# Feed-forward weights packed in alternating runs and read by a 4-D pattern

## The chip, the cores and the metric

The kernel runs on one core of one Trainium2 chip. The metric is the device time of one execution in microseconds; the number shown for the kernel before is the median of three runs. Beside the runs one execution was recorded by the hardware profiler, and all rows below come from that one.

## The reference

A sequence of 256 tokens of width 1024 goes through four layers of a mixer (banded attention, gated linear attention, differential attention, banded attention again) and a feed-forward part, each followed by a layer norm, and then through a second block with two more feed-forward parts, a sparse-attention and convolution mixer and a cross attention. The change touches only the feed-forward part of three of the four layers of the first block:

```
def swiglu(x, w_gate_up, w_down):
    g, u = jnp.split(x @ w_gate_up, 2, axis=-1)
    return (jax.nn.silu(g) * u) @ w_down
...
    for i in range(DEPTH):
...
        h = layer_norm(DN_ALPHA * h + y, ln1_g[i], ln1_b[i])
        h = layer_norm(DN_ALPHA * h + swiglu(h, ffn_w_gate_up[i], ffn_w_down[i]), ln2_g[i], ln2_b[i])
```

Here x is 256 x 1024, w_gate_up is 1024 x 5632 (2816 columns of gate, 2816 of up) and w_down is 2816 x 1024, all in float32.

## The kernel before

All weights are read from one flat array in DRAM, which the host packs in the order of use (`pack_weights`). A unit of the plan is either of kind "in" (eight row tiles of 128 x 512 of a weight matrix, for x @ W) or of kind "out" (up to four row tiles of 128 x 1024, for the projection back to 1024). A unit is used in quarters of 1024 floats per partition. SP loads each quarter into a buffer `raw`; ScalarE (L268) rounds it into `wh`, of type float32r, and VectorE (L269) writes the rest, `wl` = raw - wh. An activation is likewise held as a high and a low part (`sth`, `stl` for a layer's input, `gth`, `gtl` for the gated hidden values), transposed, so that it can be the stationary operand.

Each product is then three matmuls into one PSUM bank (`mm3`): wh with the high activation (L280), wl with the high activation (L282), wh with the low activation (L284). The weights are the moving operand, 512 columns for each matmul:

```
        for o, w in zip(outs, whs):
            nc.tensor.matmul(o, xh, w, start=first, stop=False)
```

`lin` does this for the "in" units into a bank `lin`, `lin_out` for the "out" units into two banks `acc`, one for each half of the 1024 columns. In the feed-forward part of a layer there are 11 "in" units (5 of gate, 5 of up, and one that has the last 256 columns of both) and 22 row tiles of w_down. The two token tiles of 128 go through the network as two streams that use the same split weights, the second some quarters behind the first.

The order on each engine is set by a planner at the end of the file: it plays all instructions through with rough durations that depend on the number of elements and on the engine, takes the most urgent ready one, and hands the order to the framework, which draws the waits.

The keys of the units of the layers' feed-forward parts are of the form ((i, "f"), kind, j), with i the layer; those of other units have a string or a plain number in the first place.

## Time and profile before

| | |
|---|---|
| median of 3 runs | 1971.57 us (1969.64 to 1972.45) |
| profiled execution, from its first to its last instruction | 1969.9 us |
| PE (TensorE matmuls) busy | 1945.0 us, 99% |
| DVE (VectorE) busy | 1169.3 us, 59% |
| ACT (ScalarE) busy | 927.4 us, 47% |
| DMA, weights | 607 transfers of up to 512 KB, 175 GB/s over the span |

[...] What a matmul takes away from the others is the distance between starts, and a row of a timeline gives the start in its first column. "xN" rows of a timeline merge N instructions. [...]

The feed-forward parts of layers 1, 2 and 3 stand, with a little of the neighbouring work of the other token tile between them, at 454.8 to 654 us, 767.6 to 968 us and 1083.7 to 1281.6 us of the span.

### The profile page before, as it was taken

Reading aid. Unit: us, or ns where it says so; the run is one execution under the profiler, and the core shown is the slowest. Engines: PE = TensorE matmul, PEld = TensorE weight load, DVE = VectorE, ACT = ScalarE, POOL = GpSimd, SP = SyncE. Lnnn points to the kernel's source line nnn. Section 1 sums busy time; section 2 is a strip of 40 time slices with the busy share of each in tenths; the row PEclk is TensorE's granted clock in tenths of the full one; section 3 lists DMA queues with packets and bytes.
Section 4 is the critical chain, followed back from the end, with each engine's and each line's share of the span. In section 5 each row is a group of like instructions: output and inputs, shape, how many; then the busy total and the mean of one; then the engine's idle time right before and its main releaser. Section 6 shows DMA issues by size and latency. Waiting matters only on the chain.

```text
span 1969.9 us, 23888 instructions
## 1 busy us (share of the span) xinstructions
PE 1945.0 (99%) x8998; PEld 1546.9 (79%) x8998; DVE 1169.3 (59%) x1687; ACT 927.4 (47%) x1332; POOL 48.6 (2%) x71
## 2 busy tenths in 40 slices
PE   8999999999999999999999999999999999999998
PEld 6788887678888777888877888878887788788886
DVE  5566456557555768545755655664467857556454
ACT  5445445444444555444554444444444545555442
POOL 0000000000000000000000000000001000000000
PEclk9999999999999999999999999999999999999999
DMA  9436555645555434655543655465545355536562
GB/s 287 150 139 209 181 191 154 193 148 198 186 183 182 171 129 162 222 183 181 183 143 135 217 186 184 150 225 181 186 171 183 113 197 193 163 116 206 180 186 70
DMA packets 103293, 345.59 MB, mean 175 GB/s; under 512 B 13369, under 2 KB 20473, under 8 KB 103178
## 3 DMA queue, kind: packets, MB, share of 16 engines
q1 hardware_dynamic: 103178, 344.07, 51.7%
q8 instruction: 70, 1.15, 0.2%
q14 instruction: 45, 0.37, 0.1%
HBM read 341.01 MB, written 3.01 MB: 175 GB/s over the span
## 4 chain that ended last, share of the span: by engine, by line
PE 95%; DMA 2%; DVE 1%; ACT 1%; issue 0%; SPq 0%; DVEq 0%; POOLq 0%; ACTq 0%
PE lin L282 19%; PE lin L280 19%; PE lin L284 19%; PE acc L282 9%; PE acc L284 9%; PE acc L280 9%; PE at L326 4%; PE at L574 2%; PE lin L662 1%; PE at L599 1%; DMA raw<-in_weights_dram 1%; DMA toep<-t 1%; PE lin L753 0%; PE at L741 0%; PE lin L951 0%; DVE wl L269 0%
## 5 line engine op out<-in xcount | busy, mean ns | idle before, releaser
L269 DVE TENSOR_TENSOR wl<-raw,wh 128x1024 fp32r<-128x1024 f32 (+2 forms) x614 | 741.8, 1216 | 459.6 <-ACT wh L268 459.0
L268 ACT ACTIVATE wh<-raw 128x1024 fp32r<-128x1024 f32 (+2 forms) x614 | 644.7, 1053 | 680.9 <-PE lin L284 437.6
L280 PE MATMUL lin<-wh,sth 128*128 128x512 f32 x1696 | 677.1, 403 | 3.2 <-ACT sth L331 1.4
L282 PE MATMUL lin<-wl,sth 128*128 128x512 f32 x1696 | 671.5, 400 | 1.7 <-DVE wl L269 1.7
L284 PE MATMUL lin<-wh,stl 128*128 128x512 f32 x1696 | 669.1, 399 | 0.0
L280 PEld LDWEIGHTS lin<-wh,sth 128*128 128x128 f32 x1696 | 319.5, 188 | 78.7 <-issue 4.0
L284 PEld LDWEIGHTS lin<-wh,stl 128*128 128x128 f32 x1696 | 319.3, 188 | 77.5 <-issue 4.9
L282 PEld LDWEIGHTS lin<-wl,sth 128*128 128x128 f32 x1696 | 319.4, 189 | 76.8 <-issue 4.8
L282 PE MATMUL acc<-wl,gth 128*128 128x512 f32 x752 | 251.7, 401 | 0.1
L280 PE MATMUL acc<-wh,gth 128*128 128x512 f32 x752 | 248.5, 399 | 0.2 <-ACT gth L331 0.2
L284 PE MATMUL acc<-wh,gtl 128*128 128x512 f32 x752 | 248.3, 398 | 0.0
L284 PEld LDWEIGHTS acc<-wh,gtl 128*128 128x128 f32 x752 | 141.2, 188 | 33.7 <-issue 1.3
L282 PEld LDWEIGHTS acc<-wl,gth 128*128 128x128 f32 x752 | 140.8, 189 | 32.5 <-issue 1.4
L280 PEld LDWEIGHTS acc<-wh,gth 128*128 128x128 f32 x752 | 139.8, 188 | 31.9 <-issue 1.0
L326 PE MATMUL at<-ident,t 128*128 128x128 f32 x604 | 100.4, 273 | 4.5 <-DVE t L534 1.5
L326 PEld LDWEIGHTS at<-ident,t 128*128 128x128 f32 x604 | 75.2, 140 | 28.3 <-ACT t L613 4.1
L331 ACT ACTIVATE gth<-at 128x512 fp32r<-128x512 f32 (+1 forms) x98 | 55.4, 566 | 65.8 <-PE at L326 65.7
L555 DVE TENSOR_TENSOR t<-t,lin 128x512 f32<-128x512 f32 x60 | 41.2, 687 | 74.7 <-PE lin L284 74.7
L347 POOL TENSOR_TENSOR sm<-sm,mhalf 128x1 f32<-128x1 f32 (+2 forms) x42 | 35.8, 852 | 1672.6 <-DVE sm L474 952.1
L332 DVE TENSOR_TENSOR gtl<-at,gth 128x512 fp32r<-128x512 f32 (+1 forms) x98 | 64.1, 654 | 20.2 <-ACT gth L331 17.0
L585 ACT ACTIVATE p<-p,sm 128x128 f32<-128x128 f32 (+1 forms) x112 | 49.6, 444 | 52.4 <-DVE sm L583 52.4
L552 ACT ACTIVATE t<-lin 128x512 f32<-128x512 f32 x60 | 35.9, 598 | 49.8 <-PE lin L284 49.5
(158 smaller groups left out, 911.2 us busy)
## 6 DMA issues: line engine op xcount, KB each, us to landing
raw<-in_weights_dram SPq DMA_DIRECT2D x607, 512.0 KB, 3.5
b<-toep SPq DMA_DIRECT2D x40, 128.0 KB, 4.1
bc<-in_ln_g_dram SPq DMA_DIRECT2D x8, 512.0 KB, 3.7
bc<-in_ln_b_dram SPq DMA_DIRECT2D x8, 512.0 KB, 5.9
toep<-t SPq DMA_DIRECT2D x2, 768.0 KB, 10.4
bc<-in_ffn_post_g_dram SPq DMA_DIRECT2D x2, 512.0 KB, 3.6
p<-in_mem_dram SPq DMA_DIRECT2D x2, 512.0 KB, 6.6
out_dram<-h SPq DMA_DIRECT2D x4, 256.0 KB, 2.0
```

What stands on the lines that cost most here:

```text
L268: nc.scalar.activation(hi[:, c], src[:, c], AF.Copy)
L269: nc.vector.tensor_sub(lo[:, c], src[:, c], hi[:, c].bitcast(F32))
L280: nc.tensor.matmul(o, xh, w, start=first, stop=False)
L282: nc.tensor.matmul(o, xh, w, start=False, stop=False)
L284: nc.tensor.matmul(o, xl, w, start=False, stop=last)
L326: self.nc.tensor.transpose(b[:, k], src[:, k * 128:(k + 1) * 128], self.ident)
L331: self.nc.scalar.activation(hi, b[:, :n], AF.Copy)
L332: self.nc.vector.tensor_sub(lo, b[:, :n], hi.bitcast(F32))
L552: nc.scalar.activation(gate[j], acc, AF.Silu)
L555: nc.vector.tensor_mul(s, s, acc)
L574: nc.tensor.matmul(banks[e][:, i, :nk], qT[ps, pr, :], kT(ps, pr, nk), start=True, stop=True)
L585: nc.scalar.activation(P[:, hh, :nk], P[:, hh, :nk], AF.Exp, bias=nm[:, hh:hh + 1], accum_out=sm[:, hh:hh + 1])
```

## The change

For the units whose key belongs to the feed-forward part of layer 1, 2 or 3 the host permutes the columns of each block of 512 before it writes the flat array: the block is cut into runs of 4 (layer 1), 16 (layer 2) or 2 floats (layer 3), the even runs go to its first 256 columns and the odd runs to its last 256. On the chip the moving operand of these matmuls is read by a pattern of four dimensions (partition, run pair, half, place in the run), which takes a run from the first half, then a run from the second half, and so on, so that the array sees the columns in their natural order. The transfers, the splits, the stationary operands and the outputs keep their shapes. Comments are also taken out, which moves line numbers: L280, L282 and L284 become L298, L300 and L302.

```
+RUN = {1: 4, 2: 16, 3: 2}
+
+
+def run_of(key):
+    return RUN.get(key[0][0], 0) if isinstance(key, tuple) and isinstance(key[0], tuple) else 0
+
+
+def halved(m, run):
+
+    return m.reshape(m.shape[:-1] + (-1, 256 // run, 2, run)).swapaxes(-3, -2).reshape(m.shape)
...
         blk = blk.reshape(128, -1)
+        if run_of(key):
+            blk = halved(blk, run_of(key))
         n = u.qcols * u.dma_q
...
-    def mm3(self, outs, xh, xl, whs, wls, first, last):
+    def mm3(self, outs, xh, xl, whs, wls, first, last, run=0):
         nc = self.nc
+        if run:
+            whs, wls = ([w.rearrange("p (h g j) -> p g h j", h=2, j=run) for w in ws] for ws in (whs, wls))
+            outs = [o.rearrange("p (g h j) -> p g h j", h=2, j=run) for o in outs]
...
-                self.mm3([acc[:, :n]], st[0][:, kt], st[1][:, kt], [wh[:, s]], [wl[:, s]], kt == 0, kt == 7)
+                self.mm3([acc[:, :n]], st[0][:, kt], st[1][:, kt], [wh[:, s]], [wl[:, s]], kt == 0, kt == 7,
+                         run_of(key))
...
-                self.mm3_out(gt, a, accs, c, wh, wl, first and a == 0, last and a == u.nq - 1)
+                self.mm3_out(gt, a, accs, c, wh, wl, first and a == 0, last and a == u.nq - 1, run_of(key))
...
-    def mm3_out(self, gt, a, accs, c, wh, wl, first, last):
+    def mm3_out(self, gt, a, accs, c, wh, wl, first, last, run):
...
-                 first, last)
+                 first, last, run)
```

In the built program the moving operand of the changed matmuls has, behind the partitions, the steps and counts [4, 64] [256, 2] [1, 4] in layer 1, [16, 16] [256, 2] [1, 16] in layer 2 and [2, 128] [256, 2] [1, 2] in layer 3, in floats; the output, whose four dimensions lie one behind the other, is again one run of 512. The order of instructions on each of the five engines is the one of before. Only PE has new waits: at 27 places, 9 in each of the three layers, the first matmul into a `lin` bank now also waits for a count of PE's own semaphore.

The following rows are PE's at the first use of a run of 2, before; the `lin` banks are PSUM banks of the two token tiles, `sth` and `stl` the high and low part of their input.

```order
L284 MATMUL lin_8983<-wh_8986,stl_1881_8638 128x512
L280 MATMUL lin_9014<-wh_8871,sth_1914_8784 128x512
L282 MATMUL lin_9014<-wl_8872,sth_1914_8784 128x512
L284 MATMUL lin_9014<-wh_8871,stl_1915_8785 128x512
L280 MATMUL lin_9014<-wh_8871,sth_1914_8784 128x512
L282 MATMUL lin_9014<-wl_8872,sth_1914_8784 128x512
```

And these stand there now, with the one wait that is new.

```order
L302 MATMUL lin_8983<-wh_8986,stl_1881_8638 128x512
L298 MATMUL lin_9014<-wh_8871,sth_1914_8784 128x512 [waits PE_49]
L300 MATMUL lin_9014<-wl_8872,sth_1914_8784 128x512
L302 MATMUL lin_9014<-wh_8871,stl_1915_8785 128x512
L298 MATMUL lin_9014<-wh_8871,sth_1914_8784 128x512
L300 MATMUL lin_9014<-wl_8872,sth_1914_8784 128x512
```

No instruction has moved; the wait is for an earlier matmul of the same engine, by the counts of the built program 29 matmuls back at this place, and 11, 29 or 40 back at the 27 places.

## Rows read from the trace of the kernel before

**Rows 1.** Page: busy us per engine, then busy tenths and clock by slices.
```profile
PE 1945.0 (99%) x8998; PEld 1546.9 (79%) x8998; DVE 1169.3 (59%) x1687; ACT 927.4 (47%) x1332; POOL 48.6 (2%) x71
...
PE   8999999999999999999999999999999999999998
...
PEclk9999999999999999999999999999999999999999
```

**Rows 2.** Windows of the three stretches: width, busy (count) by engine, clock, DMA.
```profile
core 0: us, PE busy (x) PEld busy (x) DVE busy (x) ACT busy (x) POOL busy (x), PEclk, DMA share, GB/s
454.00:654.00 200.00, 200.00 (x895) 161.82 (x894) 117.00 (x125) 89.37 (x100) 1.48 (x2) 1.00 0.53 187
767.00:968.00 201.00, 201.00 (x898) 162.42 (x897) 117.06 (x124) 89.91 (x100) 1.92 (x2) 1.00 0.54 189
1083.00:1282.00 199.00, 199.00 (x889) 160.89 (x888) 115.48 (x125) 90.54 (x104) 3.44 (x3) 1.00 0.52 184
```

**Rows 3.** Waits of PE, whole span: us in total, times, longest.
```profile
PE at L326 <- DMA h<-in_x_dram: 5.0, 2, 3.8
PE at L599 <- ACT p L585: 2.3, 1, 2.3
PE lin L282 <- DVE wl L269: 1.7, 3, 1.0
```

**Rows 4.** Timeline of PE in the first stretch: start, duration.
```profile
575.66 0.40 PE L280 MATMUL lin<-wh,sth 128*128 128x512 f32 x1
575.90 0.39 PE L282 MATMUL lin<-wl,sth 128*128 128x512 f32 x1
576.13 0.40 PE L284 MATMUL lin<-wh,stl 128*128 128x512 f32 x1
576.36 0.39 PE L280 MATMUL lin<-wh,sth 128*128 128x512 f32 x1
```

**Rows 5.** Timeline of PE just before 48 us.
```profile
46.00 0.63 PE L282 MATMUL lin<-wl,sth 128*128 128x512 f32 x1
46.42 0.63 PE L284 MATMUL lin<-wh,stl 128*128 128x512 f32 x1
46.85 0.63 PE L280 MATMUL lin<-wh,sth 128*128 128x512 f32 x1
47.28 0.63 PE L282 MATMUL lin<-wl,sth 128*128 128x512 f32 x1
```

**Rows 6.** Windows around those matmuls.
```profile
44.00:48.00 4.00, 4.00 (x14) 2.58 (x13) 2.51 (x7) 3.17 (x5) 0.00 (x0) 0.57 1.03 411
48.00:52.00 4.00, 4.00 (x28) 3.52 (x28) 3.04 (x8) 3.36 (x11) 0.00 (x0) 1.00 0.95 360
```

**Rows 7.** Timeline of PE where matmuls have 200 columns.
```profile
1493.73 0.26 PE L282 MATMUL lin<-wl,sth 128*128 128x200 f32 x1
1493.83 0.28 PE L284 MATMUL lin<-wh,stl 128*128 128x200 f32 x1
1493.93 0.28 PE L280 MATMUL lin<-wh,sth 128*128 128x200 f32 x1
```

**Rows 8.** Groups by form, DVE and ACT: count, busy us, mean ns, idle before.
```profile
L787 DVE TENSOR_TENSOR t<-lin,cst 128x256 f32<-128x256 f32 x8 | 3.1, 414 | 0.0
L608 DVE COPY pt<-at 128x256 f32<-128x256 f32 x2 | 0.9, 426 | 0.1
...
L606 ACT ACTIVATE k<-at 128x512 f32<-128x512 f32 x12 | 7.1, 592 | 3.9 <-PE at L326 3.8
L606 ACT ACTIVATE pt<-at 128x512 f32<-128x512 f32 x20 | 11.9, 593 | 13.6 <-PE at L599 9.3 <-PE at L326 4.2
```

## The prediction

> **What bounds the kernel now.** I read the page first. PE is busy for 1945.0 of 1969.9 us and in every one of the 40 slices at eight or nine tenths, at the full granted clock [rows 1]; the reader is to see that no other engine comes near (DVE has 59%). A share over the whole span says little about a stage, so the busy time by stretch comes next: in the three stretches that hold the changed feed-forward parts PE is busy for all of 200, 201 and 199 us, at granted clock 1.00, while DVE is busy for 115 to 117 us and ACT for some 90 us of each, and the DMA engines for little more than half [rows 2]. The view of waits says the same from the other side: over the whole span PE's longest sums of waiting are 5.0, 2.3 and 1.7 us [rows 3], and within the three stretches it lists none. So here a nanosecond that a matmul loses lengthens the kernel by a nanosecond, and nothing that SP, ACT or DVE gains shows at all.

> What a matmul costs is the distance between two starts. In the first stretch four matmuls of 512 columns start at 575.66, 575.90, 576.13 and 576.36: 0.70 us for three, 0.233 us each [rows 4]. [...]

> **The change part by part.**

> The permuting of columns is done on the host, before the launch. The transfers have the same sizes, and `raw`, `wh` and `wl` are read and written by ACT and DVE in one run as before. Cost: nothing, and there would be cover for a price: DVE is idle for 82 to 84 us of each stretch [rows 2].

> The order does not change on any engine. The 27 new waits of PE are for matmuls that stand 11, 29 or 40 places earlier on the same in-order engine. The nearest is some 11 x 0.233 = 2.6 us back [rows 4]; it will have ended while the ten behind it were still running, and the bank's reader, which PE also has to wait for, comes later than the matmul itself. Behind a waiting matmul stands all of PE's queue, so a wait that did stall would be paid in full. If the queue ran dry at each of them, the price would be at most one lone matmul, 0.40 us as drawn [rows 4], less its 0.23 us of distance: 0.17 x 27 = 4.6 us. I take 0, because the ten matmuls between cover it.

> What is left is the reading of the moving operand. Changed matmuls in a layer: 11 "in" units x 8 row tiles x 3 = 264, and 22 row tiles x 2 halves x 3 = 132, together 396 for a token tile, 792 for both. They are 792 of the 895, 898 and 889 matmuls of the three stretches [rows 2], 2376 in all. At 0.233 us they take 185 us of each stretch. In one matmul the reader now jumps 128 times in layer 1, 32 times in layer 2 and 256 times in layer 3, where it read straight on before. The outputs are one run again, so PSUM sees no difference.

> The trace of before shows no matmul with a moving operand in pieces, so this price has to be bounded. [...] From above: the only matmuls in the trace that take their columns at half the rate are those before 48 us. They start at 46.00, 46.42, 46.85 and 47.28, 0.427 us apart [rows 5], where the granted clock is at the lower of its levels for most of the 4 us (mean 0.57, and 1.00 in the 4 us after) [rows 6]. PE had waited 2.3 us for ACT shortly before [rows 3]. If a jump cost so much that columns come at half the rate, a matmul would cost 0.427 - 0.233 = 0.194 us more: 792 x 0.194 = 154 us for each layer in which this holds. For all three it would be 461 us, but the run of 16 has only 32 jumps, and I give it no weight that the other two would not share in part.

> The nearest rows in kind are those of other engines. DVE's L787 takes 256 elements in runs of 32 on both sides and needs 414 ns, and a copy of 256 elements in one run needs 426 ns. ACT writes 512 elements to `k`, which has gaps after every 128, in 592 ns, and to `pt`, which has none, in 593 ns [rows 8]. Jumps are free there, to within a few ns for 4 to 8 jumps. [...] I take 0 ns for all three runs, with the half rate for the run of 2 as the upper end that I keep for the range.

> [...]

> The sum: 1969.9 us of the profiled execution, plus 0 for the host's permuting, 0 for the waits and 3 x 792 x 0 for the reads. The runs' median lies 1.7 us above the profiled span, so the forecast for a median is 1971.6 us. About 0.2% (4 us) is what a measurement of this kernel can tell from no change.

> **The rivals.**

> First, the run of 2 halves the rate of columns in layer 3, and layers 1 and 2 stay as they are. [...] Time: 1971.6 + 154 = 2126 us; if the 20 ns come on top, 792 x 0.020 = 16 us more, 2142 us.

> Second, each jump costs a column's slot whatever the run, as an address unit that has to carry into the next dimension would. At 0.417 ns a jump, 128, 32 and 256 jumps cost 53, 13 and 107 ns: 792 x 0.173 us = 137 us, 2109 us, of which layer 1 would have 42, layer 2 11 and layer 3 85 us. For it: nothing but that all three loops are short. Against it: the rows of DVE and ACT [rows 8].

> [...]

> That the change does not do what it says is excluded: the built program has the broken patterns on all 2376 moving operands.

> **How the numbers follow.** I give 0.47 to the forecast of no change, with a range of its own of 1968 to 1976 us; 0.26 to the half rate in layer 3; 0.14 to a price for each jump; 0.10 to the small price for each line; 0.03 to a gain that I cannot explain. The last is the chance of faster, the first that of the same, and the three rivals together, 0.50, that of slower; they are split over times far apart, so the likeliest single time is still 1971.6 us. The range goes from 1967 to 2145 us: it takes in the forecast and the three rivals at the sizes worked out. Outside are a gain, a jump that costs two slots, and a half rate in more than one layer, together under 0.2.

> **What would show it.** Right: in each of the three stretches matmuls of 512 columns still start 0.233 us apart, the stretches are still 200, 201 and 199 us long, and no wait of PE on itself is listed. The first rival shows as a distance of about 0.43 us in the third stretch alone, which then is near 350 us long, with DVE and ACT busy for the same us as before. [...] Waits that do cost would show as 27 gaps of PE before a matmul at L298 with `lin`. The prediction is wrong if any of the three distances is over 0.235 us.

## The result

The changed kernel takes 2067.24 us (median of four runs, 2063.99 to 2067.98) against 1971.44 us for the one before in the same comparison: a ratio of 1.0483, 95% interval 1.0467 to 1.0499. It is slower by 96 us, inside the stated range but far from the 1971.6 us that was named as the likeliest.

The page of the kernel after, first the span, then the busy time of each engine and the slices, answers to [rows 1].

```profile
span 2064.8 us, 23897 instructions
...
PE 2040.2 (99%) x8998; PEld 1557.1 (75%) x8998; DVE 1170.5 (57%) x1687; ACT 929.2 (45%) x1332; POOL 48.7 (2%) x71
...
PE   8999999999999999999999999999999999999998
...
PEclk9999999999999999999999999999999999999999
```

PE is as full as before, at the same granted clock, with the same 8998 matmuls; DVE and ACT have the busy time of before to within 2 us. So it is not waiting that has grown, but what a matmul takes. The windows of the three stretches (width, busy time and count by engine, clock, DMA) answer to [rows 2]; the stretches have the same work and are now this long:

```profile
454.00:668.00 214.00, 214.00 (x891) 162.83 (x890) 116.52 (x123) 90.60 (x100) 1.48 (x2) 1.00 0.53 175
782.00:988.00 206.00, 206.00 (x895) 164.44 (x895) 116.74 (x124) 89.41 (x99) 1.92 (x2) 1.00 0.56 184
1103.00:1377.00 274.00, 274.00 (x890) 166.96 (x889) 116.25 (x125) 90.71 (x105) 3.44 (x3) 1.00 0.41 135
```

They were 200, 201 and 199 us. The timeline of PE (start, duration), from each stretch in turn, answers to [rows 4]:

```profile
575.50 0.42 PE L300 MATMUL lin<-wl,sth 128*128 128x512 f32 x1
575.75 0.42 PE L302 MATMUL lin<-wh,stl 128*128 128x512 f32 x1
576.00 0.42 PE L298 MATMUL lin<-wh,sth 128*128 128x512 f32 x1
...
850.81 0.40 PE L298 MATMUL lin<-wh,sth 128*128 128x512 f32 x1
851.05 0.40 PE L300 MATMUL lin<-wl,sth 128*128 128x512 f32 x1
851.29 0.40 PE L302 MATMUL lin<-wh,stl 128*128 128x512 f32 x1
...
1200.19 0.50 PE L300 MATMUL lin<-wl,sth 128*128 128x512 f32 x1
1200.52 0.50 PE L302 MATMUL lin<-wh,stl 128*128 128x512 f32 x1
1200.85 0.50 PE L298 MATMUL lin<-wh,sth 128*128 128x512 f32 x1
```

The starts are 0.25, 0.24 and 0.33 us apart. Over all neighbouring pairs of changed matmuls the medians are 252 ns for runs of 4, 240 ns for runs of 16 and 327 ns for runs of 2, where all three were 233 ns. Summed over the 792 matmuls of each layer, the distance from a start to the next start grew by 14.6, 5.5 and 74.7 us, together 94.8 us; over all other matmuls it went from 1401.4 to 1401.6 us. That is the whole difference of the two spans, 94.9 us.

PE's waits answer to [rows 3], and no wait of PE on itself is among them:

```profile
PE at L345 <- DMA h<-in_x_dram: 5.6, 2, 3.8
PE at L618 <- ACT p L604: 2.4, 1, 2.4
PE lin L300 <- DVE wl L284: 1.7, 3, 1.0
```

### The profile page after: what moved, and what is told of

The parts are those of the page before. It is cut to its first block, busy times and chain, and to the rows that moved or that the text cites. A ratio compares the mean times of both kernels' runs of the same rounds, so it can differ in the third digit from the quotient of the medians.

```text
span 2064.8 us, 23897 instructions
## 1 busy us (share of the span) xinstructions
PE 2040.2 (99%) x8998; PEld 1557.1 (75%) x8998; DVE 1170.5 (57%) x1687; ACT 929.2 (45%) x1332; POOL 48.7 (2%) x71
## 4 chain that ended last, share of the span: by engine, by line
PE 95%; DMA 2%; DVE 1%; ACT 1%; issue 0%; SPq 0%; DVEq 0%; POOLq 0%; ACTq 0%
PE lin L298 20%; PE lin L300 20%; PE lin L302 19%; PE acc L300 9%; PE acc L302 9%; PE acc L298 9%; PE at L345 4%; PE at L593 2%; PE lin L681 1%; PE at L618 1%; DMA raw<-in_weights_dram 1%; DMA toep<-t 1%; PE lin L772 0%; PE at L760 0%; PE lin L970 0%; DVE wl L284 0%
## 5 line engine op out<-in xcount | busy, mean ns | idle before, releaser
L284 DVE TENSOR_TENSOR wl<-raw,wh 128x1024 fp32r<-128x1024 f32 (+2 forms) x614 | 741.7, 1216 | 517.4 <-ACT wh L283 516.8
L298 PE MATMUL lin<-wh,sth 128*128 128x512 f32 x1696 | 700.7, 417 | 2.7 <-ACT t L632 1.2
L300 PE MATMUL lin<-wl,sth 128*128 128x512 f32 x1696 | 694.6, 414 | 1.7 <-DVE wl L284 1.7
L302 PE MATMUL lin<-wh,stl 128*128 128x512 f32 x1696 | 693.7, 414 | 0.0
L302 PEld LDWEIGHTS lin<-wh,stl 128*128 128x128 f32 x1696 | 321.2, 189 | 96.1 <-issue 4.9
L298 PEld LDWEIGHTS lin<-wh,sth 128*128 128x128 f32 x1696 | 321.7, 190 | 95.2 <-issue 4.7
L300 PEld LDWEIGHTS lin<-wl,sth 128*128 128x128 f32 x1696 | 321.6, 190 | 95.0 <-issue 4.8
L300 PE MATMUL acc<-wl,gth 128*128 128x512 f32 x752 | 262.5, 416 | 0.1
L298 PE MATMUL acc<-wh,gth 128*128 128x512 f32 x752 | 260.0, 416 | 0.2 <-ACT gth L350 0.2
L302 PE MATMUL acc<-wh,gtl 128*128 128x512 f32 x752 | 259.8, 414 | 0.0
L302 PEld LDWEIGHTS acc<-wh,gtl 128*128 128x128 f32 x752 | 142.3, 190 | 43.0 <-issue 1.3
L300 PEld LDWEIGHTS acc<-wl,gth 128*128 128x128 f32 x752 | 141.8, 190 | 42.6 <-issue 1.6
L298 PEld LDWEIGHTS acc<-wh,gth 128*128 128x128 f32 x752 | 140.9, 190 | 41.0 <-issue 1.0
```

The costliest lines, as they stand in the source:

```text
L284: nc.vector.tensor_sub(lo[:, c], src[:, c], hi[:, c].bitcast(F32))
L300: nc.tensor.matmul(o, xh, w, start=False, stop=False)
L302: nc.tensor.matmul(o, xl, w, start=False, stop=last)
```

## The experiments

In what follows a distance is the median time between the starts of two neighbouring matmuls of 512 columns with the same pattern, and a line is a name for four neighbouring floats of one partition, counted from the start of a block (16 bytes). A pattern stands as steps and counts in floats, the innermost last. Six of the nine kernels (all but those of the waits alone, of layer 3 alone and of all weights) ran once, so of them only distances within their one trace are read. Every code block shows only the part that matters.

**The waits alone.** Runs of 256 make the reads straight, and leave the 27 new waits in the program. For this the lengths of run give way to a table with three entries for each part: how the columns of a block lie in memory, in which order they are read, and how large each dimension is (h the half of the block, g the pair of runs, j the place in the run).

```
-RUN = {1: 4, 2: 16, 3: 2}
...
+READ = {
+    (1, 'f'): ('hgj', 'ghj', {'h': 2, 'g': 1, 'j': 256}),
+    (2, 'f'): ('hgj', 'ghj', {'h': 2, 'g': 1, 'j': 256}),
+    (3, 'f'): ('hgj', 'ghj', {'h': 2, 'g': 1, 'j': 256}),
+}
```

> Runs of 256: the even run is the first half of a block and the odd run the second, so the moving operands are straight again, while the 27 new waits of PE on itself stay as in the changed kernel. If the price lies in the broken reads alone: as before, 1971.5 us, ratio 1.000, matmuls of 512 columns 233 ns apart in all stretches. If the waits or the other form of the program carry a part: over 1975 us, with gaps at the 27 places; if they carried all of it, 2067 us.

Measured: 1973.92 us, ratio 1.0001 (0.9988 to 1.0014), and 233 ns in all three stretches, which take 186.3, 185.9 and 186.0 us for their 792 matmuls. The third stretch, now with straight reads, is as long as before:

```profile
1083.00:1282.00 199.00, 199.00 (x891) 160.90 (x891) 115.63 (x126) 91.05 (x104) 3.44 (x3) 1.00 0.54 182
```

The waits cost nothing that can be seen.

**Layer 3 alone.**

```
-RUN = {1: 4, 2: 16, 3: 2}
...
+READ = {
+    (3, 'f'): ('hgj', 'ghj', {'h': 2, 'g': 128, 'j': 2}),
+}
```

> Only layer 3 keeps its broken reads (runs of 2); layers 1 and 2 are as before. If each layer pays for its own matmuls: 792 x (327 - 233) ns = 74 us, so 2046 us, ratio 1.038, and the distance in the third stretch stays 327 ns while the other two go back to 233. If the three patterns act on each other (buffers or streams that run late): off that by several us, near 2067 or near 2030 us.

Measured: 2047.14 us, ratio 1.0379 (1.0353 to 1.0405), 327 ns in the third stretch. Its windows show the first two stretches at their old length and the third as after:

```profile
454.00:654.00 200.00, 199.96 (x893) 161.54 (x892) 116.78 (x124) 89.09 (x100) 1.48 (x2) 1.00 0.56 186
767.00:968.00 201.00, 201.00 (x899) 162.54 (x898) 117.18 (x125) 89.92 (x100) 1.92 (x2) 1.00 0.57 188
1083.00:1357.00 274.00, 274.00 (x890) 166.96 (x889) 116.37 (x125) 90.86 (x104) 3.44 (x3) 1.00 0.40 135
```

Each layer pays for its own matmuls, and the prices add.

**Six lengths of run.** The six feed-forward parts of the kernel each get another length, with 792 matmuls each.

```
+    (0, 'f'): ('hgj', 'ghj', {'h': 2, 'g': 2, 'j': 128}),
+    (1, 'f'): ('hgj', 'ghj', {'h': 2, 'g': 4, 'j': 64}),
+    (2, 'f'): ('hgj', 'ghj', {'h': 2, 'g': 8, 'j': 32}),
+    (3, 'f'): ('hgj', 'ghj', {'h': 2, 'g': 32, 'j': 8}),
+    'f1': ('hgj', 'ghj', {'h': 2, 'g': 256, 'j': 1}),
+    'f2': ('hgj', 'ghj', {'h': 2, 'g': 16, 'j': 16}),
```

Here f1 and f2 are the two feed-forward parts of the second block.

> Six feed-forward parts, each with another length of run, 792 matmuls each: 128, 64, 32 and 8 floats in layers 0 to 3, 1 float in the first and 16 in the second feed-forward part of the second block. Theory of lines (the price is set by how often a new line of 16 bytes is entered, 1.25 ns each where that is slower than the columns): all runs from 4 up enter 128 lines and differ little from straight reads, at most as the run of 16 did, 240 ns; the run of 1 enters a line for each of 512 columns, 512 x 1.25 = 640 ns. Theory of jumps (each break of the pattern costs a fixed 0.15 to 0.37 ns): 2, 4, 8 and 16 ... jumps give 234, 235, 237 ns for runs of 128, 64, 32, then 247 to 256 ns for the run of 8 (64 jumps), 240 for 16 and 310 to 420 ns for the run of 1 (512 jumps).

Measured: 233, 233 and 236 ns for runs of 128, 64 and 32, 245 ns for 8 and 240 ns again for 16. But the run of 1, for which one theory had 640 ns (its 1.25 ns a line is near the 327 / 256 = 1.28 of the run of 2) and the other 310 to 420 ns, is the fastest of all, and faster than straight reading. Its timeline:

```profile
1401.28 0.38 PE L312 MATMUL lin<-wl,sth 128*128 128x512 f32 x1
1401.49 0.38 PE L314 MATMUL lin<-wh,stl 128*128 128x512 f32 x1
1401.71 0.38 PE L310 MATMUL lin<-wh,sth 128*128 128x512 f32 x1
1401.92 0.38 PE L312 MATMUL lin<-wl,sth 128*128 128x512 f32 x1
```

The distance is 0.215 us (median 216 ns). For what 512 columns would take with nothing added there is an estimate: the matmuls of [rows 5] come 0.427 us apart at a granted clock of 0.50, by their window (width, busy time and count by engine, clock, DMA),

```profile
46.00:47.00 1.00, 1.00 (x4) 0.81 (x3) 1.00 (x4) 0.96 (x1) 0.00 (x0) 0.50 1.03 410
```

and half of that is 213 ns at a clock of 1.00, if the whole distance goes with the clock. The run of 1 is next to nothing above it. It jumps 512 times, and every column lies in another line than the one before it. Both theories of that run fall.

**Six other orders.** The same table is set to other orders. Instead of its entries, the list gives the patterns that come of them in the built program.

```
layer 0:  [4, 128] [1, 2] [2, 2]     in each line 0 2 1 3
layer 1:  [2, 2] [4, 128] [1, 2]     two floats of every line, then the other two
layer 2:  [4, 2] [8, 64] [1, 4]      every other line
layer 3:  [1, 4] [4, 128]            one float of every line, four times
f1:       [1, 2] [2, 256]            every other float, twice
f2:       [4, 32] [128, 4] [1, 4]    runs of 4 round four quarters
```

> Six other patterns, 792 matmuls each. Layer 0: within each group of four floats (a line of 16 bytes) the order 0 2 1 3, lines in order. Layer 1: the first two floats of every line, lines in order, then the last two. Layer 2: every other line whole, then the rest. Layer 3: one float of every line, four times over. First part of the second block: every other float, twice over. Second: runs of 4 going round the four quarters of a block. Theory of lines: 233, 327, 233 to 252, 640, 327, 252 ns for a matmul. Theory of jumps: 420, 327, 252, 420, 420, 252 ns. Theory of the two far halves (the price comes from going to and fro between places 1024 bytes apart): 233 ns in the first five, and over 233 only in the last.

Measured: 233, 453, 233, 461, 453 and 270 ns. The theory of far halves falls with the second, fourth and fifth, the theory of jumps with the first (0 2 1 3 leaves its place at three of four columns, and costs nothing). The theory of lines has the sign of each right, but not the sizes: two floats of a line at a time cost as much as one. The timeline of the second (near 600 us), and of the fourth (near 1450 us):

```profile
600.16 0.65 PE L312 MATMUL lin<-wl,sth 128*128 128x512 f32 x1
600.61 0.65 PE L314 MATMUL lin<-wh,stl 128*128 128x512 f32 x1
601.06 0.65 PE L310 MATMUL lin<-wh,sth 128*128 128x512 f32 x1
...
1450.43 0.66 PE L312 MATMUL lin<-wl,sth 128*128 128x512 f32 x1
1450.90 0.66 PE L314 MATMUL lin<-wh,stl 128*128 128x512 f32 x1
1451.36 0.66 PE L310 MATMUL lin<-wh,sth 128*128 128x512 f32 x1
```

Here an estimate was formed from the distances. It takes every second column of a pattern by itself, and counts how often such a column lies in another line than the one before it: 128 times in straight reading, 256 times with every other float and with one or two floats of a line, 64 times in the run of 1 to and fro. Such a new line, which the expectations further on call a fetch, is given 1.8 ns, from 233 / 128 = 1.82, 453 / 256 = 1.77 and 461 / 256 = 1.80 ns, and below 216 ns, the smallest distance measured, the count is not to go. It has 230 ns for the first and the third of these orders, where 233 were measured, but also for the last, which took 270 ns; and for the runs of 2, which took 327 ns, it is too high with 461. How PE reads the columns no view of the trace shows; the estimate is made to fit distances.

**Distance, and what the estimate gives.**

Again the list gives the patterns of the built program.

```
layer 0:  [4, 4] [16, 32] [1, 4]     runs of 4, step 64 bytes
layer 1:  [4, 8] [32, 16] [1, 4]     step 128 bytes
layer 2:  [4, 16] [64, 8] [1, 4]     step 256 bytes
layer 3:  [1, 2] [2, 128] [256, 2]   one column from each half, in steps of two
f1:       [8, 64] [1, 4] [4, 2]      to and fro between neighbouring lines
f2:       [1, 128] [128, 4]          runs of 1 round four quarters
```

> Layers 0, 1, 2: runs of 4 that step by 64, 128 and 256 bytes and come back for the next ones. Layer 3: columns in pairs that lie 1024 bytes apart, pair after pair in order within two floats (first float of both halves, second float of both halves came already in the run of 1; here the halves are every other float). First part of the second block: runs of 1 to and fro between two lines that lie side by side. Second: runs of 1 going round the four quarters of a block. [...] Theory of pairs (two columns that come from two places are read faster than two neighbours): 216 ns in layer 3, 233 ns or more for the lines side by side, 216 ns for the quarters.

Measured: 227, 248 and 277 ns; 233 ns; 216 ns; 283 ns. The estimate has 230 ns for layer 3 (128 new lines) and 216 ns for the neighbouring lines (64), where the theory of pairs had 216, and 233 or more. For the quarters it is too high again, 461 ns, and the theory of pairs, with 216, too low. The neighbouring lines (first) and the quarters (second):

```profile
1419.98 0.38 PE L314 MATMUL lin<-wh,stl 128*128 128x512 f32 x1
1420.19 0.38 PE L310 MATMUL lin<-wh,sth 128*128 128x512 f32 x1
1420.41 0.38 PE L312 MATMUL lin<-wl,sth 128*128 128x512 f32 x1
1420.63 0.38 PE L314 MATMUL lin<-wh,stl 128*128 128x512 f32 x1
...
1900.61 0.45 PE L312 MATMUL lin<-wl,sth 128*128 128x512 f32 x1
1900.90 0.45 PE L314 MATMUL lin<-wh,stl 128*128 128x512 f32 x1
1901.18 0.45 PE L310 MATMUL lin<-wh,sth 128*128 128x512 f32 x1
```

The first three show a second price, which the estimate (230 ns for each) does not have: runs of 4 take each line whole, and yet pay more when the next line lies farther off, from 227 ns at 64 bytes (less than straight reading) to 277 ns at 256. The step and the number of places change together here.

**The weight load, first try, and more places at once.** The 128 stationary columns are read with a step of eight floats in some parts (`x.rearrange("p k t -> p (k t)")[:, kt::8]`); layer 2 gets [1, 64] [64, 8] and the first part of the second block [2, 64] [128, 4] [1, 2].

> In the first two thirds of the matmuls (gate and up) of layer 0, 1, 3 and of the last feed-forward part the 128 stationary columns are read with a step of 32 bytes, 128 lines instead of 32; they are then other numbers than the reference's input. Moving operands: straight in layer 0, runs of 1 in layer 1, runs of 2 in layer 3, runs of 4 in the last. Layer 2: runs of 1 going round eight places (stationary as before). First part of the second block: runs of 2 going round four quarters (stationary as before). If the 17 ns between 216 and 233 are fetches that the weight load takes from a moving operand that has none to spare: about 285 ns in layer 0 and still about 216 ns in layer 1, whose fetches take half the time. If weight load and moving operand do not meet: 233 and 216 ns. [...]

Measured: 246 ns in layer 0 (straight) and 242 ns in layer 1 (runs of 1), where 285 and 216, or 233 and 216, were expected; 339 and 255 ns for the runs of 2 and 4. Both sides miss, so this could not tell them apart. The trace draws the weight load itself (PEld) with 328 ns in layer 0, longer than a matmul's distance, where it had 188 ns before; that this sets the 246 ns was not shown. The rows of the 100 us from 200 us on, before (first) and here (second):

```profile
L280 PEld LDWEIGHTS lin<-wh,sth 128*128 128x128 f32 x100 | 18.8, 188 | 4.3
L313 PEld LDWEIGHTS lin<-wh,sth 128*128 128x128 f32 x92 | 30.1, 328 | 0.7
```

The eight places took 493 ns and the runs of 2 round four quarters 447 ns. The theory of jumps, at up to 0.37 ns for each of 512 and 256 jumps, gives at most 420 and 327 ns; the estimate gives 461 ns for both (256 new lines), 32 too low and 14 too high.

**Two places at other distances.** The second place lies 252, 248, 240, 224 or 192 floats behind the first.

```
+            ap = lambda w: bass.AP(tensor=w.tensor, offset=w.offset, ap=[list(w.ap)[0], [j, 256 // j], [step, 2], [1, j]])
```

> Runs of 4 to and fro between two places that lie 1008, 992, 960, 896 and 768 bytes apart (layers 0 to 3 and the first feed-forward part of the second block) instead of 1024, and runs of 2 between places 1008 bytes apart in the last. The columns are not packed for it, and the two places overlap, so some columns are read twice and others not at all: the products are not the reference's there. [...] If any far jump costs them: 252 ns in all five. [...]

Measured: 243 ns at 1008, 992, 960 and 896 bytes, 252 ns at 768 (and 1024); 347 ns for the runs of 2, where about a fifth of the distances are 327 or less. So it is not 252 ns in all five: any of these distances costs 10 ns, and the two multiples of 256 bytes some 9 ns more. The runs of 2 took 327 ns at 1024 bytes, 20 less than here: these runs too pay for where their second place lies.

**The weight load, second try.** Fewer stationary columns (`COLS = {(0, 'f'): 32, (1, 'f'): 32, 'f1': 32, 'f2': 64}`), or all of them with a step of two.

> The weight load beside the moving operand, in the gate and up matmuls of six feed-forward parts. For the six inner ones of eight row tiles, layer 0 (straight), layer 1 (runs of 1) and the first part of the second block (runs of 2) have 32 instead of 128 stationary columns, the last part (straight) 64: the other rows of those products are left out. Layers 2 (straight) and 3 (runs of 1) read all 128, but with a step of two floats, 64 lines instead of 32, and so not the reference's input. If the 17 ns are fetches that the weight load takes from a straight moving operand, which has none to spare: 220 ns in layer 0, 225 in the last, 250 in layer 2, 216 in layers 1 and 3, some 323 for the runs of 2. If they have nothing to do with the weight load: 233 ns in layers 0, 2 and the last, 216 in 1 and 3, 327 for the runs of 2.

Measured: 232 ns with 32 stationary columns, 233 with 64, 229 with the step of two, all straight; 216 ns for the runs of 1 in both forms; 327 ns for the runs of 2. A quarter of the stationary columns gives nothing back, so the 17 ns between straight reading and runs of 1 do not come with the number of stationary columns. Why the step of two gives 229 is open. With 32 columns:

```profile
200.42 0.40 PE L316 MATMUL lin<-wl,sth 128*32 128x512 f32 x1
200.66 0.40 PE L318 MATMUL lin<-wh,stl 128*32 128x512 f32 x1
200.89 0.40 PE L314 MATMUL lin<-wh,sth 128*32 128x512 f32 x1
201.12 0.39 PE L316 MATMUL lin<-wl,sth 128*32 128x512 f32 x1
```

**All weights in runs of 1.** The kernel before, with every moving weight block packed as its even columns, then its odd ones.

```
+        if u.width >= 64:
+            n = min(u.width, 512)        # even columns of a block, then its odd ones
+            blk = blk.reshape(128, -1, n // 2, 2).transpose(0, 1, 3, 2)
         blk = blk.reshape(128, -1)
...
+        whs, wls = ([w.rearrange("p (h g) -> p g h", h=2) for w in ws] for ws in (whs, wls))
+        outs = [o.rearrange("p (g h) -> p g h", h=2) for o in outs]
```

> Every unit that feeds a moving operand, in all layers and both blocks, is packed as even columns then odd columns of a block and read back by runs of 1. If the 216 ns of the run of 1 come from the reading alone: 7296 matmuls of 512 columns gain 17 ns each, 124 us, so 1847 us, ratio 0.937, 216 ns in every stretch. If they came from that one place in the kernel, 233 ns elsewhere: near 1971 us. If splits or transfers now come late: between, 1870 to 1900 us, with waits of PE for wl or wh that the kernel before has not.

Measured: 1864.04 us (median of five), ratio to the kernel before 0.9455 (0.9439 to 0.9471): it beats both kernels, the changed one by 203 us. The distance is 216 ns in all stretches. Its page and a piece of its timeline in the stretch of the first layers:

```profile
span 1859.3 us, 23907 instructions
...
PE 1825.6 (98%) x8998; PEld 1552.7 (84%) x8998; DVE 1167.4 (63%) x1687; ACT 924.5 (50%) x1332; POOL 48.5 (3%) x71
```

```profile
499.76 0.38 PE L289 MATMUL lin<-wh,stl 128*128 128x512 f32 x1
499.98 0.38 PE L285 MATMUL lin<-wh,sth 128*128 128x512 f32 x1
500.19 0.38 PE L287 MATMUL lin<-wl,sth 128*128 128x512 f32 x1
500.41 0.38 PE L289 MATMUL lin<-wh,stl 128*128 128x512 f32 x1
```

Of the 124 us expected it brings 107 to 111. Between two such matmuls the sum of distances fell by 114.5 us, from 1627.1 to 1512.6; the 465 that are followed by something else gained nothing (139.8 to 142.1 us), nor did the rest (192.6 to 194.0). Within these sums PE sits idle for some 9 us more, a little at each of many places:

```profile
PE at L331 <- ACT sm L723: 3.6, 1, 3.6
PE at L331 <- DVE t L539: 2.6, 4, 1.7
PE lin L287 <- DVE wl L272: 2.3, 3, 1.1
```

## Why the prediction was right or wrong

**The bound was read rightly.** PE never waited in the three stretches, so each nanosecond of a matmul came out in the span: 94.8 us in the distances, 94.9 us in the span. The count of 792 matmuls a layer held. (DVE is idle for 83 to 84 us of each stretch by [rows 2], not 82 to 84; nothing hangs on it.)

**The free parts were free.** The host's permuting changed nothing on DVE or ACT, and the waits on PE itself cost nothing, as the runs of 256 show.

**The step that failed** is "I take 0 ns for all three runs". They cost 19, 7 and 94 ns a matmul, 14.6, 5.5 and 74.7 us. The 0 was taken from DVE and ACT with runs of 32 and 128 [rows 8] as the nearest in kind. For PE such long runs are nearly free as well (236 and 233 ns); the rows said nothing of runs shorter than 32, and that was where the question lay. The matmuls at the lower clock [rows 5] were the nearer evidence, which the prediction uses for its upper end alone: their 512 columns come 0.427 us apart at a granted clock of 0.50, so that 213 ns at 1.00 is the estimate and some 20 of the 233 ns lie above it. The runs of 1 then showed what these are: with another order of reading, and nothing else changed, 17 of the 20 ns go (216 ns). The prediction gave a gain 0.03 and could not explain one.

**The row of 200 columns** [rows 7] was evidence at hand as well. Its three starts are 0.100 us apart, but they stand at the start of a group; over all neighbouring pairs the median is 111 ns. In the version with runs of 1 the matmuls of 200 columns are still 112 ns apart, with the columns in runs of 1, while those of 512 fall from 233 to 216. Before (first two rows) and with runs of 1 (last two):

```profile
1494.27 0.28 PE L280 MATMUL lin<-wh,sth 128*128 128x200 f32 x1
1494.38 0.27 PE L282 MATMUL lin<-wl,sth 128*128 128x200 f32 x1
...
1410.23 0.28 PE L285 MATMUL lin<-wh,sth 128*128 128x200 f32 x1
1410.34 0.28 PE L287 MATMUL lin<-wl,sth 128*128 128x200 f32 x1
```

So the order of reading that takes 17 ns off 512 columns takes nothing off 200. What holds these was not tried.

**The first rival** had the place (layer 3), but not the size: 94 ns and not 194. Half the rate does come with two floats of a line in order, 453 ns; the runs of 2, which soon come back to a line that they have just read from, stay at 327 ns. The 20 ns on top in its time of 2142 us no run shows by themselves: they are 233 ns less an estimate, and what the runs showed is 233 ns for straight reads and 216 ns for runs of 1. The second rival had all layers paying, which they do, but in the ratio 4 to 1 to 8; measured is 2.7 to 1 to 13. No run shows its 0.417 ns a jump either: the order 0 2 1 3 jumps at three of four columns and stays at 233 ns, and the three layers paid 0.15, 0.22 and 0.37 ns a jump (19, 7 and 94 ns for 128, 32 and 256). A small price for each line, which had 0.10, is out: the run of 2 pays 94 ns. The chance of slower, 0.50, was spread over the rivals, and the range reached to them; the likeliest single case, 0.47, was wrong. That 2067 us lies inside the range is therefore luck: the range was drawn to take in rivals at 2109 and 2126 to 2142 us, none of which came, and the true sum lay between them and the forecast. By the prediction's own sign, a distance over 0.235 us, it failed in all three layers (0.252, 0.240 and 0.327 us).

**What is shown, and what is only an estimate.** Shown: the price lies in the order of reading alone (the same program with straight reads costs nothing), adds layer by layer, is set neither by the number of jumps nor by the waits, and has a gain on the other side; a quarter of the stationary columns changes neither the 233 ns of straight reads nor the 327 ns of runs of 2. The count of new lines in every second column is an estimate from distances. Straight reads, every other float and one or two floats of a line set its 1.8 ns; of the patterns that ran after it, one column from each half in steps of two (233 ns) and the neighbouring lines (216 ns) came within 3 ns of it, and the runs of 2 round four quarters within 14 ns (447 for 461). It fails for the runs of 2 (327 and 347 for 461) and for single floats round four quarters (283 for 461), lies 32 ns off for eight places (493 for 461), and has no price of distance. Open is the price of distance: runs of 4 cost 227 ns at steps of 64 bytes, 248 at 128, 277 at 256, 270 at 512, 252 between halves 1024 bytes apart and 243 at 896 to 1008. That is the 19 ns of layer 1 and the 7 ns of layer 2, 20 of the 95 us, and no run here says where it comes from. Nor is it one number: in layer 1 the distances run from 243 ns or less (a tenth of them) to 259 or more (another tenth), and grouping them by the stationary tile of the matmul that follows takes away some two thirds of their variance. No experiment followed that up.

## What to carry to other kernels

Where PE never waits, the distance between starts of its matmuls is the kernel; compare it with that of the same columns in another order of reading or at another granted clock (here 233 ns with 216, and with half of 427), and ask in what order the operand is read before calling a difference a price of the instruction. Bound an access pattern by rows of the same engine at the same rate, or by an experiment; long runs on other engines say nothing of short ones. Weights that the host packs anyway can be packed for the order of reading: with float32r operands at a granted clock of 1.00, even columns and odd columns in separate lines gave 5.5% (1864 us against 1971 us).
